# A seven-product pair kernel: negated products preset into PSUM by ScalarE, three banks in place of four, and another order of the products

## The chip, the cores and the metric

The kernel runs on one core of a Trainium2 chip. Times are device microseconds (us) of one execution. A comparison of two kernels uses runs of both on the same chip. PE is TensorE (matrix products), ACT is ScalarE, DVE is VectorE, POOL is GpSimd and SP is SyncE, which issues most transfers. Products are written to PSUM, an accumulator memory of eight banks per partition, from which ACT and DVE read.

## The reference

One layer of a hybrid decoder is computed for 512 prompt tokens and 64 sample tokens, so 576 token columns in all, with width 1024:

```python
h = _rmsnorm(x, norm1_g) * (1.0 + sc1) + sh1
proj = h @ w_in          # b_gate, c_gate, xa, q, k, v, ga, gb
ya = (b_gate * uc) @ w_conv_out          # uc: causal conv of c_gate * xa
yb = o @ w_attn_out                      # o: windowed attention of q, k, v
mixed = jax.nn.sigmoid(ga) * ya + jax.nn.sigmoid(gb) * yb
x = x + g1 * (mixed @ w_mix_out)
h2 = _rmsnorm(x, norm2_g) * (1.0 + sc2) + sh2
a, val = jnp.split(h2 @ w_up, 2, axis=-1)
ac, new_ffn = _causal_conv(a, ffn_buf, ffn_conv_w)
x = x + g2 * ((jax.nn.gelu(ac, approximate=False) * val) @ w_down)
```

The results are the normed outputs and the new convolution and key/value states. All arrays are float32.

## The kernel before, in words

Activations lie transposed in the core's memory: 128 features in the partitions, 576 tokens in the columns (`NT`, its half `HT` is 288). A weight tile covers 1024 input features and 128 output features. Every float32 operand is split in two: a high part, a rounded copy that ACT makes, and a low part, the remainder, that DVE makes (`split`, lines 135 to 138). A product is then three passes on PE: high by high, high by low, low by high.

The stages follow one another in the text of the kernel: norm and modulation, q, k, v, the short convolution with the attention woven in (`fill`, `tick`, lines 174 to 187), its output projection, the gates, the attention projection and merge, the mix projection, the second norm, the ConvFFN in three runs of weight tiles (`FCH`, line 28), each followed by its share of the down projection, and the final norm.

An ordinary product (`product`, lines 206 to 211) puts all 576 columns into one tile of two PSUM banks (`mmps`, a pool of two such tiles), in column groups of 256 and 320 (`GRP`, line 23; `halves`). Single banks come from `aux`, a pool of four.

Gates (16 weight tiles, 8 pairs) and most of the up projection (18 pairs of a value tile and a gate tile) are done by `pair_product` (lines 334 to 377). It treats the two weight tiles, their two input halves of 512 features and the two column halves of 288 as a two by two matrix product, and gets it with seven products of half size rather than eight. Sums and differences of the weights are made by DVE one pair ahead (`pair_weights`, lines 283 to 327: A, B, C, D stand for the split parts, such as `ah` for the high part of A and `al` for the low part), those of the activations once (`PairOperands`). Each of the seven parts is 12 matrix instructions of 288 columns into one bank. Parts write X, Y, Z, X, W, Y, Z. X and W are `aux` banks, Y and Z are two `mmps` tiles, each used in its first half bank alone. Between the parts, ACT copies part 1 and part 3 out of PSUM (`p1`, `p5`), DVE forms `u` and `v` (differences with `p1`), and the four results are formed by the functions `out_a0` to `out_b1` that the caller gives.

For the gates (`sigmoid_pair`, lines 1200 to 1219) these take the sigmoid. For the ConvFFN (`FfnPair.run`, lines 1520 to 1541) `value0` keeps X in PSUM, `value1` is a DVE subtraction, `gate0` and `gate1` write the padded gate tile `u` for the causal convolution, the last 64 columns by POOL. The convolution of one pair runs beside the products of the next: `first_tap` (ACT), `taps` (two DVE operations), `gelu` (ACT), `times` (DVE and POOL), `high` and `low` (the split of the result).

From the gates on, the instructions of PE, ACT and DVE are pinned to the order in which the text issues them (`InOrder`, lines 101 to 115, `pinned`), up to the last down projection (line 1737) with a break in the merge and mix stages. `in_turn` (lines 329 to 332) and `beside_pair` (lines 1561 to 1571) say after which part of a pair each split of the next weights and each convolution step of the pair before is issued. So an instruction that waits holds up all that stand behind it on its engine. Where two instructions touch the same tile, the tile framework puts a semaphore wait between them.

Of the kernel before, what the change touches and what calls it, by code (L numbers as in the profile page):

```python
# [12 lines left out]
AF = mybir.ActivationFunctionType  # L13
ALU = mybir.AluOpType
# [7 lines left out]
NT = SEQ + 64  # L22
GRP = [(0, 256), (256, 576)]
# [11 lines left out]
W_BUFS = 4  # L35
S_BUFS = 5
HT = NT // 2
NORM2 = 4, 0, 3, 1, 3
WARM = 2, 5
CND, CNS, CIND, CSL, CEND = 0, 256, 768, 772, 776  # L40
# [29 lines left out]
def step_kernel(ctx: ExitStack, tc: tile.TileContext, ins: dict, outs: list):  # L70
    nc = tc.nc
# [18 lines left out]
    def slot(s, dt=F32, shape=None):  # L90
        return ap_.tile(shape or [P, NT], dt, tag="a", name=nm(s))

    def mmps():
        return pm.tile([P, 1024], F32, tag="mm", name=nm("mm"))

    def aux():
        return pa.tile([P, 512], F32, tag="aux", name=nm("aux"))
# [16 lines left out]
    pe, act, dve, pool = (InOrder(e) for e in (nc.tensor, nc.scalar, nc.vector, nc.gpsimd))  # L114
    pinned += [pe, act, dve, pool]
    matmul, transpose = pe.matmul, pe.transpose
# [3 lines left out]
    def pf(ps):  # L120
        return ps[:, 256:832]
# [69 lines left out]
            if next(filler[0], True):  # L191
                filler.clear()

    def kstep(dst, w, xs, k, groups=(0, 1)):

        hi, lo = w
        xh, xl = xs[k]
        first, last = k == 0, k == len(xs) - 1
        for wt, x, st, sp_ in ((hi(k), xh, first, False), (hi(k), xl, False, False), (lo(k), xh, False, last)):
            for g in groups:  # L200
                matmul(dst[g], wt, x[:, GRP[g][0] : GRP[g][1]], start=st, stop=sp_)

    def halves(ps):
        return ps[:, 256:512], ps[:, 512:832]

    def product(w, xs):
        ps = mmps()
        for k in range(len(xs)):
            kstep(halves(ps), w, xs, k)
            tick()  # L210
        return pf(ps)

    def product_g(w, xs, g, bank=None, between=None):

# [113 lines left out]

    def in_turn(t):

        order = {0: "sums1 ah al", 2: "dh dl sums2", 3: "bh bl", 4: "ch cl"}
        return {at: (lambda names=names: [t[n]() for n in names.split()]) for at, names in order.items()}

    def pair_product(w, x, steps, out_a0, out_a1, out_b0, out_b1):

        X, Y, Z, W = (t[:, :HT] for t in (aux(), mmps(), mmps(), aux()))
        keep, uv = slot("p15"), slot("uv")
        p1, p5, u, v = keep[:, :HT], keep[:, HT:], uv[:, :HT], uv[:, HT:]  # L340

        def part(at, bank, wn, xn_, more=False):

            (hi, lo), xs = w[wn], x[xn_]
            for k in range(4):
                xh, xl = xs[k]
                passes = (hi(k), xh), (hi(k), xl), (lo(k), xh)
                for n, (wt, xx) in enumerate(passes):
                    matmul(
                        bank, wt, xx, start=not more and k + n == 0, stop=k + n == 5,  # L350
                        skip_group_check=more,
                    )
                tick()
            if at in (1, 3):
                act.copy(p1 if at == 1 else p5, bank)
            elif at == 2:
                dve.tensor_tensor(out=u, in0=Y, in1=p1, op=ALU.subtract)
            elif at == 4:
                out_a0(X)
            elif at == 6:  # L360
                dve.tensor_tensor(out=v, in0=Y, in1=p1, op=ALU.subtract)
                out_b0(v, W, ALU.add)
                out_b1(v, p5, ALU.subtract)
            elif at == 7:
                out_a1(Z, u, ALU.subtract)
            if at in steps:
                steps[at]()

        if 0 in steps:
            steps[0]()  # L370
        part(1, X, "a0", "x00")
        part(2, Y, "s2", "t2")
        part(3, Z, "s1", "n1")
        part(4, X, "a1", "x10", True)
        part(5, W, "b1", "n4")
        part(6, Y, "s3", "n3", True)
        part(7, Z, "s4", "x11", True)

    def kpm(w, m0, k0=0, nk=NK):
        return w[k0 * P : (k0 + nk) * P, m0 : m0 + P].rearrange("(k p) m -> p k m", p=P)  # L380
# [79 lines left out]
    part = cp.tile([P, 2, 8], F32, tag="part1", name="part1")  # L460
# [236 lines left out]
    for j in (2, 0, 1):  # L697
        t = slot("kT")
# [37 lines left out]
    for i in range(5):  # L736
        ps = aux()
# [11 lines left out]
    for i in (3, 4):  # L749
# [3 lines left out]
        t = slot("kout", shape=[P, 256])  # L753
# [21 lines left out]
    def queries(t, ps=None):  # L775
# [52 lines left out]
        out=sel,  # L828
        in0=snk.rearrange("p (h g) -> p h g", h=4),
        in1=ind.unsqueeze(1).to_broadcast([P, 4, 4]),  # L830
        op=ALU.mult,
# [331 lines left out]
    for m in range(NK):  # L1163
        if m in (5, 6):
            src, dst = ((ins["cache_k_win"], nks), (ins["cache_v_win"], nvs))[m - 5]
# [34 lines left out]
    def sigmoid_pair(w, steps):  # L1200

        sa, sb = slot("sg"), slot("sg")

        def a0(ps):
            act.activation(sa[:, :HT], ps, AF.Sigmoid)

        def a1(x, y, op):
            dve.tensor_tensor(out=sa[:, HT:], in0=x, in1=y, op=op)
            act.activation(sa[:, HT:], sa[:, HT:], AF.Sigmoid)

        def b0(x, y, op):
            dve.tensor_tensor(out=sb[:, :HT], in0=x, in1=y, op=op)

        def b1(x, y, op):
            dve.tensor_tensor(out=sb[:, HT:], in0=x, in1=y, op=op)
            act.activation(sb, sb, AF.Sigmoid)

        pair_product(w, made["op"], steps, a0, a1, b0, b1)
        return [sa, sb]
# [80 lines left out]
    def residual(ps, xt, blk, c0=0, c1=NT):  # L1300

        p1 = min(c1, 512)
        dve.scalar_tensor_tensor(
            out=xt[:, c0:p1], in0=ps[:, : p1 - c0], scalar=modT[:, blk, 0:1], in1=xt[:, c0:p1],
            op0=ALU.mult, op1=ALU.add,
        )
        if c1 > 512:
            t = sp.tile([P, 64], F32, tag="rt", name=nm("rt"))
            dve.tensor_tensor(
                out=b8(t), in0=b8(ps[:, p1 - c0 :]), in1=bc(modT[:, blk, 1:9]), op=ALU.mult  # L1310
            )
            dve.tensor_tensor(out=sv(xt), in0=sv(xt), in1=t, op=ALU.add)
# [196 lines left out]
    class FfnPair(FfnTile):  # L1509
# [10 lines left out]
        def run(self, steps):  # L1520
            self.u = u = padded()

            def value0(ps):
                self.x0 = ps

            def value1(x, y, op):
                self.x1 = y
                dve.tensor_tensor(out=y, in0=x, in1=y, op=op)

            def gate0(x, y, op):  # L1530
                dve.tensor_tensor(out=u[:, 2 : 2 + HT], in0=x, in1=y, op=op)

            def gate1(x, y, op):
                n = 512 - HT
                dve.tensor_tensor(out=u[:, 2 + HT : 514], in0=x[:, :n], in1=y[:, :n], op=op)
                nc.gpsimd.tensor_tensor(
                    out=b10(u)[:, :, 2:10], in0=b8(x[:, n:]), in1=b8(y[:, n:]), op=op
                )
                self.state()

            pair_product(self.w, made2["op"], steps, value0, value1, gate0, gate1)
# [19 lines left out]
    def beside_pair(p, t):  # L1561

        none = lambda: None
        f = lambda n: t[n] if t else none
        g = lambda n: getattr(p, n) if p else none
        return {
            0: [f("ah"), g("first_tap"), f("sums1"), f("al"), g("taps")],
            1: [f("dh"), f("bh"), g("gelu")],
            2: [f("dl"), f("sums2"), f("bl"), g("times")],
            4: [f("ch"), g("high"), f("cl"), g("low")],  # L1570
        }

# [114 lines left out]
    for m0, m1 in FCH:  # L1687
# [24 lines left out]
        if m1 < NF:  # L1712
            pairs = {m1: FfnPair(m1)}
            steps = None
            ps = [mmps() for _ in range(2)]
            n = m1 - m0
            for k0, k1 in ((0, n - 2), (n - 2, n)):
                for j in range(2):
                    for k in range(k0, k1):
                        kstep(halves(ps[j]), wd[j], fa, k)  # L1720
            wd[2] = split_w(down_load(2, m0, m1))
            for j in range(2):
                residual(pf(ps[j]), x1[j], 40 + j)
            for m in range(2, NK):
                if m + 1 < NK:
                    wd[m + 1] = split_w(down_load(m + 1, m0, m1))
                acc_m = product(wd[m], fa)
                if m == 4:
                    steps = in_turn(pairs[m1].prepare())
                    steps[0]()  # L1730
                elif m > 4:
                    steps[m - 3]()
                if m == NK - 1:
                    pairs[m1 + 1] = FfnPair(m1 + 1)
                residual(acc_m, x1[m], 40 + m)
            continue
# [32 lines left out]
        for k0, k1 in ((0, n - 2), (n - 2, n)):  # L1769
            for j in range(2):  # L1770
                for k in range(k0, k1):
                    kstep(halves(ps[j]), wd[j], fa, k)
        w = split_w(down_load(2, m0, m1))
        for j in range(2):
            residual(pf(ps[j]), x1[j], 40 + j)
            summed(j)
        for m in range(2, NK - LATE):
            acc_m = product(w, fa)
# [64 lines left out]
```

## Time and profile before

| What | Value |
| --- | --- |
| Time, median of 3 runs | 1001.54 us (1001.21 to 1002.3) |
| Span of the profiled execution, first to last instruction | 999.2 us |
| PE busy | 983.2 us, 98% of the span |
| DVE busy | 672.2 us, 67% |
| ACT busy | 449.6 us, 45% |
| POOL busy | 100.4 us, 10% |
| Chain that ended last, share of PE | 88% |
| Mean granted TensorE clock | 0.998 |

The profile is of one execution. Its page gives busy time by engine, the chain of work that ended last, and groups of instructions with their count, busy time, mean duration in ns and the idle time before them. The name before the arrow is the tile written, those behind it are read; `mm` and `aux` are PSUM tiles. Nearly all rows of PE, ACT and DVE carry the line of the helper that records them (L109), so tiles and shapes tell them apart. Windows give the busy time of each engine within a stretch, with the number of instructions, the granted clock, and the share and rate of the DMA engines. A timeline row gives start, duration, engine and, in brackets, idle time before it with what ended it.

### The profile page before, as it was taken

To read this page: it belongs to the slowest core of one execution; us is meant where nothing else is said; L and a number is where in the kernel's file an instruction comes from. 1 tells how busy PE (TensorE), PEld (TensorE's weight loads), DVE (VectorE), ACT (ScalarE), POOL (GpSimd) and SP (SyncE) were. 2 spreads that over 40 slices of the span, in tenths; PEclk is the share of its full clock that TensorE was granted. 3 is DMA by queue.
4 is the path that set the end of the run, shared out by engine and by line. 5 is a ranking of instruction groups with operands and counts; after the bars stand their busy time and mean duration, and the time that the engine had idled before them with its cause. 6 is when DMAs were issued, how large, how long until landed. Compare 5 with 4: busy or idle time off the path is not lost.

```text
span 999.2 us, 18724 instructions
## 1 busy us (share of the span) xinstructions
PE 983.2 (98%) x7516; PEld 942.1 (94%) x7516; DVE 672.2 (67%) x1243; ACT 449.6 (45%) x837; POOL 100.4 (10%) x271
## 2 busy tenths in 40 slices
PE   7999999999999999999999999999999999999997
PEld 6799999999989889999889999999999999999997
DVE  5637666666563367888454568896569995579954
ACT  5354545444544225545232347554225553235453
POOL 2222111100010000000000021011001110001120
PEclk9999999999999999999999999999999999999999
DMA  9983322333423822235972302233233222323302
GB/s 305 320 247 95 107 84 78 93 110 111 141 65 88 289 97 85 86 103 156 342 230 73 107 6 79 65 85 106 85 95 95 86 85 86 106 67 100 110 9 95
DMA packets 173481, 119.18 MB, mean 119 GB/s; under 512 B 6887, under 2 KB 160846, under 8 KB 173106
## 3 DMA queue, kind: packets, MB, share of 16 engines
q1 hardware_dynamic: 169954, 107.00, 35.1%
q0 software_dynamic: 3296, 10.73, 3.4%
q8 instruction: 59, 0.97, 0.4%
q14 instruction: 28, 0.23, 0.1%
q10 hardware_dynamic: 144, 0.26, 0.1%
HBM read 109.17 MB, written 7.35 MB: 117 GB/s over the span
## 4 chain that ended last, share of the span: by engine, by line
PE 88%; DVE 5%; ACT 2%; DMA 2%; issue 2%; SPq 0%; POOL 0%; POOLq 0%; DVEq 0%; ACTq 0%
PE mm L109 64%; PE aux L109 21%; PE aux L1104 2%; PE aux L1019 1%; DMA ad<-in_w_ada 1%; DVE wlo L109 1%; DMA raw<-in_w_in 1%; ACT whi L109 1%; SPq L385 0%; DVE raw L109 0%; DVE cy L109 0%; ACT y L109 0%; DVE uv L109 0%; DVE tl L109 0%; DVE fl L109 0%
## 5 line engine op out<-in xcount | busy, mean ns | idle before, releaser
L109 ACT ACTIVATE whi<-raw 128x1024 fp32r<-128x1024 f32 (+3 forms) x166 | 168.1, 1024 | 200.8 <-PE mm L109 106.9
L109 DVE TENSOR_TENSOR wlo<-raw,whi 128x1024 fp32r<-128x1024 f32 (+3 forms) x166 | 195.3, 1183 | 48.3 <-ACT whi L109 46.2
L109 PE MATMUL mm<-hh,whi 128*128 128x256 f32 (+2 forms) x560 | 127.6, 304 | 0.5 <-ACT hh L109 0.5
L109 PE MATMUL mm<-hh,wlo 128*128 128x256 f32 (+2 forms) x560 | 122.1, 295 | 0.0
L109 PE MATMUL mm<-hl,whi 128*128 128x256 f32 (+2 forms) x560 | 121.0, 295 | 0.1
L109 PEld LDWEIGHTS mm<-hh,whi 128*128 128x128 f32 x560 | 91.6, 188 | 8.1 <-issue 6.6
L109 PEld LDWEIGHTS mm<-hl,whi 128*128 128x128 f32 x560 | 93.7, 188 | 0.7 <-DVE hl L109 0.5
L109 PEld LDWEIGHTS mm<-hh,wlo 128*128 128x128 f32 x560 | 94.2, 188 | 0.0
L109 DVE SCALAR_TENSOR_TENSOR x<-mm,modT,x 128x512 f32<-128x512 f32 (+1 forms) x33 | 22.6, 686 | 70.6 <-PE mm L109 70.5
L109 PE MATMUL mm<-fl,whi 128*128 128x256 f32 (+1 forms) x304 | 65.4, 296 | 0.0
L109 PE MATMUL mm<-fh,whi 128*128 128x256 f32 (+1 forms) x304 | 64.8, 295 | 0.3 <-DVE rt L109 0.3
L109 PE MATMUL mm<-fh,wlo 128*128 128x256 f32 (+1 forms) x304 | 64.7, 294 | 0.0
L109 PE MATMUL mm<-th,whi 128*128 128x288 f32 x208 | 61.6, 296 | 0.7 <-DVE uv L109 0.7
L109 PE MATMUL mm<-th,wlo 128*128 128x288 f32 x208 | 61.4, 295 | 0.5 <-DVE wlo L109 0.5
L109 PE MATMUL mm<-tl,whi 128*128 128x288 f32 x208 | 61.2, 294 | 0.0
L109 PEld LDWEIGHTS mm<-fh,whi 128*128 128x128 f32 x304 | 50.6, 188 | 0.5 <-PE mm L109 0.5
L109 PEld LDWEIGHTS mm<-fh,wlo 128*128 128x128 f32 x304 | 51.0, 188 | 0.0
L109 PEld LDWEIGHTS mm<-fl,whi 128*128 128x128 f32 x304 | 50.9, 188 | 0.0
L109 PE MATMUL aux<-2h,whi 128*128 128x288 f32 (+2 forms) x160 | 47.3, 295 | 0.8 <-ACT p L109 0.8
L109 PE MATMUL aux<-2h,wlo 128*128 128x288 f32 (+2 forms) x160 | 47.2, 295 | 0.0
L109 PE MATMUL aux<-2l,whi 128*128 128x288 f32 (+2 forms) x160 | 47.0, 294 | 0.0
L870 ACT ACTIVATE s<-s,nmx 128x256 f32<-128x256 f32 (+1 forms) x72 | 34.1, 475 | 25.5 <-DVE nmx L867 17.4
(310 smaller groups left out, 2569.8 us busy)
## 6 DMA issues: line engine op xcount, KB each, us to landing
raw<-in_w_in SPq DMA_DIRECT2D x52, 512.0 KB, 4.2
raw<-in_w_up SPq DMA_DIRECT2D x44, 512.0 KB, 3.8
ada<-in_w_ada SPq DMA_DIRECT2D x64, 256.0 KB, 6.0
ad<-in_w_ada SPq DMA_DIRECT2D x32, 256.0 KB, 6.3
raw<-in_w_down SPq DMA_DIRECT2D x16, 512.0 KB, 3.5
raw<-in_w_conv_out SPq DMA_DIRECT2D x8, 512.0 KB, 3.5
raw<-in_w_attn_out SPq DMA_DIRECT2D x8, 512.0 KB, 3.5
raw<-in_w_mix_out SPq DMA_DIRECT2D x8, 512.0 KB, 5.6
```

The costliest lines, as they stand in the source:

```text
L109: done = getattr(self.engine, name)(*args, **kwargs)
L870: nc.scalar.activation(s[x // 2][:, x % 2, :w], s[x // 2][:, x % 2, :w], AF.Exp, bias=nmx[:, x : x + 1], accum_out=den[:, x : x + 1],)
L1019: done = nc.tensor.matmul(O[HALF[par], :256], vt(i - nkt + 1 + kt)[:, hd * 64 : hd * 64 + 64], pts[kt][:, par * 256 : par * 256 + 256], st ...
L1104: done = nc.tensor.matmul(ps[32 * j : 32 * j + 32, :], cT[:, k, :], cols[k][j], start=(k == 1), stop=(k == NK - 2),)
```

## The change

- Y and Z are now the two halves of one `mmps` tile (`even_halves`): the 288 columns before column 512 and the 288 columns from it on, one half in each of its two banks. W is gone, and with X a pair uses three banks. The slots `p1`, `u` and `v` are gone; only `p5` stays.
- The parts come in a new order and go to X, Z, Y, X, Y, Z, Y. After part 1 ACT writes the negated X into Y, and the products of part 3 add onto it. After part 3 ACT writes the negated Y into Z, and part 6 adds onto that. ACT still copies Z to `p5` after part 2.
- `b0` is now complete in Y after part 7 and read by ACT: a copy into `u` for the ConvFFN (`gate0`), a sigmoid for the gates. `b1` is a DVE subtraction after part 5, `a1` a DVE addition after part 6. The last 64 columns of `gate1` move from POOL to DVE.
- In the gates, the sigmoid of `sb` is done in two halves.
- The splits of the next weights are issued in another order (`in_turn`, `beside_pair`): B before D.
- Ordinary products and the first two down projections of each run use two even column groups of 288 (`EVEN`, `whole`).

```diff
+EVEN = [(0, HT), (HT, NT)]
...
-    def kstep(dst, w, xs, k, groups=(0, 1)):
+    def kstep(dst, w, xs, k, groups=(0, 1), at=GRP):
...
-                matmul(dst[g], wt, x[:, GRP[g][0] : GRP[g][1]], start=st, stop=sp_)
+                matmul(dst[g], wt, x[:, at[g][0] : at[g][1]], start=st, stop=sp_)
...
+    def even_halves(ps):
+        return ps[:, 512 - HT : 512], ps[:, 512 : 512 + HT]
+
+    def even_step(ps, w, xs, k):
+        kstep(even_halves(ps), w, xs, k, at=EVEN)
+
+    def whole(ps):
+        return ps[:, 512 - HT : 512 + HT]
...
-        order = {0: "sums1 ah al", 2: "dh dl sums2", 3: "bh bl", 4: "ch cl"}
+        order = {0: "sums1 ah al", 2: "bh bl sums2", 3: "dh dl", 4: "ch cl"}
...
-        X, Y, Z, W = (t[:, :HT] for t in (aux(), mmps(), mmps(), aux()))
-        keep, uv = slot("p15"), slot("uv")
-        p1, p5, u, v = keep[:, :HT], keep[:, HT:], uv[:, :HT], uv[:, HT:]
+        X = aux()[:, :HT]
+        Y, Z = even_halves(mmps())
+        p5 = slot("p5")[:, :HT]
...
-            if at in (1, 3):
-                act.copy(p1 if at == 1 else p5, bank)
-            elif at == 2:
-                dve.tensor_tensor(out=u, in0=Y, in1=p1, op=ALU.subtract)
-            elif at == 4:
-                out_a0(X)
-            elif at == 6:
-                dve.tensor_tensor(out=v, in0=Y, in1=p1, op=ALU.subtract)
-                out_b0(v, W, ALU.add)
-                out_b1(v, p5, ALU.subtract)
-            elif at == 7:
-                out_a1(Z, u, ALU.subtract)
...
+        def minus(out, src):
+            act.activation(out, src, AF.Copy, scale=-1.0)
+
+        parts = [
+            (X, "a0", "x00", lambda: minus(Y, X)),
+            (Z, "s1", "n1", lambda: act.copy(p5, Z)),
+            (Y, "s2", "t2", lambda: minus(Z, Y)),
+            (X, "a1", "x10", lambda: out_a0(X)),
+            (Y, "s3", "n3", lambda: out_b1(Y, p5, ALU.subtract)),
+            (Z, "s4", "x11", lambda: out_a1(Z, p5, ALU.add)),
+            (Y, "b1", "n4", lambda: out_b0(Y)),
+        ]
...
-            act.activation(sb, sb, AF.Sigmoid)
+        def a1(x, y, op):
+            sigmoid(sb[:, HT:], sb[:, HT:])
+            dve.tensor_tensor(out=sa[:, HT:], in0=x, in1=y, op=op)
+
+        def b0(ps):
+            sigmoid(sb[:, :HT], ps)
+            sigmoid(sa[:, HT:], sa[:, HT:])
...
-            def gate0(x, y, op):
-                dve.tensor_tensor(out=u[:, 2 : 2 + HT], in0=x, in1=y, op=op)
+            def gate0(ps):
+                act.copy(u[:, 2 : 2 + HT], ps)
...
-                nc.gpsimd.tensor_tensor(
+                dve.tensor_tensor(
                     out=b10(u)[:, :, 2:10], in0=b8(x[:, n:]), in1=b8(y[:, n:]), op=op
                 )
...
-            1: [f("dh"), f("bh"), g("gelu")],
-            2: [f("dl"), f("sums2"), f("bl"), g("times")],
+            1: [f("bh"), g("gelu")],
+            2: [f("bl"), f("sums2"), f("dh"), f("dl"), g("times")],
```

More of the change, by code (lines that the diff above doesn't have):

```diff
@@ L208, in product @@
         for k in range(len(xs)):
-            kstep(halves(ps), w, xs, k)
+            even_step(ps, w, xs, k)
             tick()
-        return pf(ps)
+        return whole(ps)
     def product_g(w, xs, g, bank=None, between=None):
@@ L329, in in_turn, with part @@
     def in_turn(t):
-        order = {0: "sums1 ah al", 2: "dh dl sums2", 3: "bh bl", 4: "ch cl"}
+        order = {0: "sums1 ah al", 2: "bh bl sums2", 3: "dh dl", 4: "ch cl"}
         return {at: (lambda names=names: [t[n]() for n in names.split()]) for at, names in order.items()}
     def pair_product(w, x, steps, out_a0, out_a1, out_b0, out_b1):
-        X, Y, Z, W = (t[:, :HT] for t in (aux(), mmps(), mmps(), aux()))
-        keep, uv = slot("p15"), slot("uv")
-        p1, p5, u, v = keep[:, :HT], keep[:, HT:], uv[:, :HT], uv[:, HT:]
-        def part(at, bank, wn, xn_, more=False):
+        X = aux()[:, :HT]
+        Y, Z = even_halves(mmps())
+        p5 = slot("p5")[:, :HT]
+        def part(bank, wn, xn_, more=True):
             (hi, lo), xs = w[wn], x[xn_]
@@ L353, in part @@
                 tick()
-            if at in (1, 3):
-                act.copy(p1 if at == 1 else p5, bank)
-            elif at == 2:
-                dve.tensor_tensor(out=u, in0=Y, in1=p1, op=ALU.subtract)
-            elif at == 4:
-                out_a0(X)
-            elif at == 6:
-                dve.tensor_tensor(out=v, in0=Y, in1=p1, op=ALU.subtract)
-                out_b0(v, W, ALU.add)
-                out_b1(v, p5, ALU.subtract)
-            elif at == 7:
-                out_a1(Z, u, ALU.subtract)
-            if at in steps:
-                steps[at]()
+        def minus(out, src):
[9 more added lines that the diff above has]
+        ]
         if 0 in steps:
             steps[0]()
[L371 to L377, printed above, removed]
+        for at, (bank, wn, xn_, after) in enumerate(parts):
+            part(bank, wn, xn_, at > 1)
+            after()
+            if at + 1 in steps:
+                steps[at + 1]()
     def kpm(w, m0, k0=0, nk=NK):
@@ L1202, in sigmoid_pair, with sigmoid @@
         sa, sb = slot("sg"), slot("sg")
+        def sigmoid(out, src):
+            act.activation(out, src, AF.Sigmoid)
         def a0(ps):
[L1205 to L1212, printed above, removed]
+            sigmoid(sa[:, :HT], ps)
         def b1(x, y, op):
             dve.tensor_tensor(out=sb[:, HT:], in0=x, in1=y, op=op)
-            act.activation(sb, sb, AF.Sigmoid)
+        def a1(x, y, op):
[4 more added lines that the diff above has]
+            sigmoid(sa[:, HT:], sa[:, HT:])
         pair_product(w, made["op"], steps, a0, a1, b0, b1)
@@ L1719, in step_kernel @@
                     for k in range(k0, k1):
-                        kstep(halves(ps[j]), wd[j], fa, k)
+                        even_step(ps[j], wd[j], fa, k)
             wd[2] = split_w(down_load(2, m0, m1))
             for j in range(2):
-                residual(pf(ps[j]), x1[j], 40 + j)
+                residual(whole(ps[j]), x1[j], 40 + j)
             for m in range(2, NK):
@@ L1771, in step_kernel @@
                 for k in range(k0, k1):
-                    kstep(halves(ps[j]), wd[j], fa, k)
+                    even_step(ps[j], wd[j], fa, k)
         w = split_w(down_load(2, m0, m1))
         for j in range(2):
-            residual(pf(ps[j]), x1[j], 40 + j)
+            residual(whole(ps[j]), x1[j], 40 + j)
             summed(j)
```

## The prediction

> **What bounds the kernel now.** I read the page first, then the windows over the pair stages, then single instructions there.
>
> ```profile
> span 999.2 us, 18724 instructions
> ...
> PE 983.2 (98%) x7516; PEld 942.1 (94%) x7516; DVE 672.2 (67%) x1243; ACT 449.6 (45%) x837; POOL 100.4 (10%) x271
> ```
>
> The span is 999.2 us against a median of 1001.54, so 2.3 us lie around it; I keep these. TensorE works almost without a pause. A change pays only by closing PE gaps, and costs whatever gaps it opens. The change sits in 26 pairs of weight tiles: 8 gate pairs (from about 380 us) and 18 ConvFFN pairs (three runs of 4, 8 and 6). The windows for one pair each (columns: PE, weight loads, DVE, ACT, POOL busy, then clock):
>
> ```profile
> 413.40:424.50 11.10, 11.10 (x86) 11.10 (x86) 9.04 (x13) 5.59 (x10) 0.00 (x0) 1.00 0.34 97
> ...
> 760.30:771.40 11.10, 11.10 (x86) 11.10 (x86) 10.97 (x17) 6.35 (x9) 1.42 (x5) 1.00 0.30 86
> ...
> 805.30:816.90 11.60, 11.30 (x86) 11.09 (x85) 11.46 (x19) 5.92 (x9) 1.76 (x6) 1.00 0.32 95
> ```
>
> A pair is 84 products and takes 11.1 us, 0.132 us a product. In ConvFFN pairs DVE is as full as PE, and late in a run the pair stretches. The chain in order of time gives the pair starts:
>
> ```profile
> 783.67 3.16 PE mm L109 x24
> ...
> 794.77 3.39 PE mm L109 x24
> ...
> 806.40 3.40 PE mm L109 x24
> ...
> 818.02 3.40 PE mm L109 x24
> ```
>
> 11.10, then 11.63 and 11.62: 0.5 us lost in such a pair. With the first pair of the first run (below) I put all that a lighter DVE could win at 3.5 us.
>
> **How one wait costs.** In the first ConvFFN pair PE already waits for a ScalarE copy of 288 columns, and a little later an unhindered copy follows its products (timeline):
>
> ```profile
> 646.24 0.37 ACT L109 COPY p<-aux 128x288 f32<-128x288 f32 x1
> ...
> 646.66 0.40 PE L109 MATMUL aux<-2h,whi 128*128 128x288 f32 x1 [0.84 <-ACT p L109]
> ...
> 646.90 0.29 PE L109 MATMUL aux<-2l,whi 128*128 128x288 f32 x1
> ```
>
> ```profile
> 750.07 0.29 PE L109 MATMUL aux<-2h,wlo 128*128 128x288 f32 x1
> 750.21 0.29 PE L109 MATMUL mm<-th,whi 128*128 128x288 f32 x1
> ```
>
> ```profile
> 750.40 0.40 ACT L109 COPY p<-aux 128x288 f32<-128x288 f32 x1 [1.04 <-PE aux L109]
> 750.70 0.64 ACT L109 ACTIVATE wh<-s 128x512 fp32r<-128x512 f32 x1
> ```
>
> Read: the copy starts 0.33 us after the start of the last product (750.07), lasts 0.40, and the next ACT operation begins 0.30 after it. PE restarts 0.05 after the copy's end (646.61 to 646.66) and its second product comes 0.24 later, not 0.13. So a product group that must wait for a copy of the group directly before it starts 0.33 + 0.40 + 0.05 - 0.13 = 0.65 us late, plus 0.11 for the restart: 0.76 us.
>
> **The change, part by part.** *New waits.* Y and Z become the two halves of one tile of two banks. In the program built from the changed kernel the products wait for the last access to the tile, not to their half. In all 26 pairs, with groups G1 to G7 in the new order (X, Z, Y, X, Y, Z, Y): G2 (Z) waits for the negated copy into Y; G3 (Y) waits for that and the copy of Z to p5; G5 (Y) for the negated copy into Z; G6 (Z) for the DVE reads of Y; G7 (Y) for the DVE read of Z. Only G5 has a whole group (G4, into X) to hide behind. Before, Y, Z, X and W are four tiles, and no such wait shows. Behind each wait stands all of PE's later work, in order.
>
> What PE waits for also stands in a queue, so durations matter (groups by line and form, mean ns after the comma):
>
> ```profile
> L109 DVE TENSOR_TENSOR wlo<-raw,whi 128x1024 fp32r<-128x1024 f32 x154 | 187.5, 1221 | 48.3 <-ACT whi L109 46.2 <-PE aux L109 1.6
> L109 ACT ACTIVATE whi<-raw 128x1024 fp32r<-128x1024 f32 x154 | 161.3, 1055 | 200.5 <-PE mm L109 106.9 <-DMA raw<-in_w_down 35.4 <-DVE raw L109 22.7
> ...
> L109 DVE SCALAR_TENSOR_TENSOR y<-pad,par2T,y 128x592 f32<-128x592 f32 x44 | 36.6, 833 | 4.9 <-ACT y L109 3.9
> ...
> L109 ACT ACTIVATE y<-pad,par2T 128x592 f32<-128x592 f32 x22 | 17.4, 792 | 32.7 <-POOL sto L1082 29.8 <-DVE pad L109 2.6
> L109 DVE TENSOR_TENSOR fl<-cy,fh 128x576 fp32r<-128x576 f32 x22 | 16.5, 752 | 5.2 <-ACT fh L109 5.2
> ...
> L109 ACT ACTIVATE y<-y 128x592 f32<-128x592 f32 x22 | 15.4, 699 | 30.7 <-DVE y L109 30.7
> ...
> L109 DVE TENSOR_TENSOR uv<-mm,uv 128x288 f32<-128x288 f32 x18 | 8.1, 452 | 1.4 <-PE mm L109 1.4
> L109 DVE TENSOR_TENSOR pad<-uv,p 128x224 f32<-128x224 f32 x18 | 6.9, 386 | 0.0
> ```
>
> *A full ConvFFN pair* (12 of the 18: a neighbour before and behind). Zero is the start of the last product of the pair before. Operations of one engine overlap by about 0.08 to 0.1, as above.
> - G1's last product starts at 1.59. ACT has meanwhile: the new copy of the gate out of Y (0.33), the high half of the next A (0.63 to 1.68), the first tap (to 2.37). Only then the negated copy, 2.28 to 2.68. G2 starts at 2.73, not 1.72: 1.01 lost.
> - G2's last starts at 4.29. The p5 copy stands behind the GELU, which needs the DVE's taps: low half of A from 1.73, taps 2.87 and 3.73 to 4.56, GELU 4.60, p5 5.20 to 5.60. G3 starts at 5.65, not 4.42: 1.23 lost.
> - G3's last 7.21; the negated copy into Z, 7.54 to 7.94, lies beside G4; G5 runs on, last product 10.38. 0 lost.
> - The DVE's gate operations on Y stand behind the low halves of C and of the pair before: ACT high C 8.99 to 10.04 (it needs the end of G4), low C to 11.31, the other low half to 11.97, then 0.39 and 0.20 on Y, done at 12.40. G6 starts at 12.45, not 10.51: 1.94 lost.
> - G7 waits for the in-place DVE add on p5: 0.33 + 0.45 + 0.05 - 0.13 = 0.70 lost.
>
> With four restarts of 0.11: 5.3 us a pair, 12 pairs: 64 us.
>
> *First and last pair of a run* (6): without a pair before there are no taps or GELU ahead of p5, and nothing but low C ahead of the gate: 0.65 + 0.65 + 1.27 + 0.70 + 0.44 = 3.7, three times: 11. The last has no next weights, so nothing but the next low half: 0.65 + 0.65 + 0.78 + 0.70 + 0.44 = 3.2, three times: 10.
>
> *Gate pairs* (8):
>
> ```profile
> L109 ACT ACTIVATE sg<-aux x8: 410/412/414, 391.1 to 468.0; 128x288 f32<-128x288 f32 x8
> ```
>
> G2 and G3 at 0.76 each, G7 at 0.81. After G4 come the sigmoid (0.33), high C 0.31 later (1.05), low C on DVE (1.74 to 2.96), and only then the add on Y, 2.88 to 3.33: G6 is 1.66 + 0.11 late. 4.1 us a pair: 33 us.
>
> *DVE relief.* In ConvFFN, three operations of 0.45 leave DVE and 0.20 comes in from POOL, in gate pairs three leave: beside PE, worth the 3.5 us above at most. If PE waits anyway, they go into the waits.
>
> *Even halves in ordinary products.* 256 + 320 columns become 288 + 288:
>
> ```profile
> L109 PE MATMUL mm<-th,whi 128*128 128x288 f32 x208 | 61.6, 296 | 0.7 <-DVE uv L109 0.7
> ...
> L109 PE MATMUL mm<-fh,wlo 128*128 128x320 f32 x152 | 46.8, 308 | 0.0
> ...
> L109 PE MATMUL mm<-fh,wlo 128*128 128x256 f32 x152 | 42.6, 280 | 0.0
> ```
>
> (308 + 280)/2 = 294 against 296: nothing. SP's DMA order is unchanged. The gate copy, now after the last group, delays the last run's tail by some 0.7 us.
>
> *Unknown: ScalarE writing PSUM.* No row shows it. Nearest are the 0.37 to 0.40 us copies out of PSUM and 0.64 for 512 columns; I take 0.40, and keep 0.2 and 0.64 as ends. It lies on the path once a pair: 26 x (-0.2 to +0.24) = -5 to +6 us.
>
> **Sum:** 64 + 11 + 10 + 33 = 118, less 3.5, plus 0.7: 115. The span goes to 1114, the median to 1116.5.
>
> **Rivals.** *Waits at their floor.* If the queues of ACT and DVE have drained when a group ends (PE being slower, they might), each of four waits costs 0.76 or 0.81: 3.1 x 26 = 81, less 3.5: 1079. Against it: the splits of C are held by the end of G4 itself. 8%.
>
> *Waits by bank.* If the waits on the other half were met early, only true dependences remain: gate copy, high A, taps, p5, copy into Z, gate operations, G7. The same chain then ends at 10.66 where G7 would start at 9.64, so about 1.1 us in 12 pairs: 13, less 3.5: 1011. 3%. The Trainium skill, "PSUM — Partial Sum Buffer" (section "PSUM bank collisions raise a hardware error"), says to guard PSUM by bank and quadrant, or simply by bank, rather than by address; by it the waits between Y and Z, in two banks, are needless and this rival would hold. The trace of before agrees as far as it goes: a copy out of one bank runs beside products into another at 750.40.
>
> *Faster.* The same, and the chain fits into G7's start: DVE's relief of 1.1 us closes the 3.5 us of gaps: 998. It decides if ACT does high A before the gate copy, which its order in the built program excludes. 2%.
>
> *The clock falls.* PE would idle 5 of 16 us. If the granted clock halved for a tenth of the 26 x 11.1 us of pair products, +29: 1145; for all of them, 1400.
>
> ```profile
> 0.00:10.00 10.00, 5.45 (x28) 4.99 (x29) 3.98 (x8) 6.66 (x15) 3.24 (x14) 1.00 0.76 244
> ```
>
> Against it: 1.00 here, with PE busy 5.45 of 10. 6%. The Trainium skill, "TensorE: Matmul & The Clock Gate" (section "What's actually happening"), has the gate close after an idle window of about 3.4 us; by it gaps of at most 2 us keep the clock, and the row agrees.
>
> **Numbers.** Forecast 1116, 81%. Range 1075 to 1145: the copy's ends, the floor, a tenth of clock loss. Only waits by bank, the faster case and a large clock loss lie outside. 0.2% (2 us) is about what a measurement can tell: slower 0.97, within 0.01, faster 0.02.
>
> **What would show it.** Right: in the windows a middle ConvFFN pair at about 16.4 us with PE busy 11 to 12, a gate pair at 15.2; PE waiting for ACT's mm and p5 and for DVE's pad, p5 and sg in all 26 pairs, 1.9 us at most; DVE below 70% there; product stages unchanged. Wrong: pairs of 11 to 12 us, or waits of 0.7 us only, or a clock under 1.

## The result, and the profile after

The changed kernel takes 1131.97 us (median of 5 runs, 1130.04 to 1140.43), the kernel before 1001.54 us on the same chip. The ratio is 1.132, with a 95% interval of 1.128 to 1.135. The profiled execution is the longest of the five: 1140.43 us with a mean granted clock of 0.972; the other four have 0.981 to 0.986.

The page of the changed kernel:

```profile
span 1138.5 us, 18682 instructions
...
PE 1032.7 (91%) x7516; PEld 968.4 (85%) x7516; DVE 646.9 (57%) x1183; ACT 465.2 (41%) x889; POOL 92.2 (8%) x253
...
PEclk9999999999999989999999998899988999989899
```

PE runs the same 7516 products, but is idle for 106 us instead of 16, and its busy time has grown by 50 us: the clock row shows eights, which the kernel before has none of in its pair stages. The windows of single pairs, from one pair's first product to the next one's (columns: PE, weight loads, DVE, ACT, POOL busy, clock, DMA):

```profile
450.02:465.28 15.26, 12.17 (x86) 11.23 (x85) 8.76 (x12) 6.09 (x11) 0.00 (x0) 1.00 0.23 69
...
747.00:800.00 53.00, 52.45 (x396) 52.38 (x396) 24.92 (x41) 13.37 (x15) 0.79 (x5) 1.00 0.29 85
815.04:833.28 18.24, 14.02 (x87) 12.96 (x86) 10.70 (x16) 6.85 (x11) 1.43 (x5) 0.87 0.19 58
884.96:901.39 16.43, 12.19 (x86) 11.26 (x85) 10.70 (x16) 6.85 (x11) 1.37 (x5) 1.00 0.22 65
800.15:815.04 14.89, 12.19 (x87) 11.25 (x85) 10.06 (x16) 3.85 (x6) 0.33 (x2) 1.00 0.25 72
676.96:699.65 22.69, 15.66 (x86) 14.61 (x85) 13.81 (x22) 7.91 (x14) 0.33 (x2) 0.77 0.32 94
```

A gate pair (450) takes 15.3 us, a middle ConvFFN pair (885) 16.4, the first pair of a run (800) 14.9: 11.1 each before. The down projection between two runs (747 to 800) is nearly as full as it was. Two rows show what comes on top: a pair in which the clock falls (815) takes 18.2 us, and the very first ConvFFN pair (677) 22.7 us. Seven middle pairs are of the first kind, with 17.7 to 18.9 us. The waits of PE (total us, times, longest):

```profile
PE mm L110 <- DVE pad L110: 26.1, 17, 1.8
PE mm L110 <- ACT p L110: 19.5, 26, 1.1
PE mm L110 <- ACT mm L110: 19.4, 25, 4.8
PE mm L110 <- DVE sg L110: 16.2, 16, 2.2
PE mm L110 <- DVE p L110: 9.9, 18, 0.6
```

None of these rows stands in the profile before. Their sum is 91 us, less than the 139 by which this execution's span is longer than that of the kernel before. A row counts from the end of the last product, which lies some 0.16 us behind the point where the next one would have started (the 0.84 us below make a group 1.00 us late): 16 us more in 102 waits. The restarts (0.11 each, 11 us) and the clock come on top.

The sizes within one pair, from the timeline of PE in the pair at 884.96 (start, duration; in brackets the idle time and what ended it):

```profile
886.41 0.29 PE L110 MATMUL aux<-2h,wlo 128*128 128x288 f32 x1
...
887.54 0.40 PE L110 MATMUL mm<-th,whi 128*128 128x288 f32 x1 [0.84 <-ACT mm L110]
...
889.10 0.29 PE L110 MATMUL mm<-th,wlo 128*128 128x288 f32 x1
...
890.46 0.40 PE L110 MATMUL mm<-th,whi 128*128 128x288 f32 x1 [1.06 <-ACT p L110]
...
895.22 0.29 PE L110 MATMUL mm<-2h,wl 128*128 128x288 f32 x1
...
897.31 0.40 PE L110 MATMUL mm<-2h,whi 128*128 128x288 f32 x1 [1.79 <-DVE pad L110]
...
898.86 0.29 PE L110 MATMUL mm<-2h,wlo 128*128 128x288 f32 x1
...
899.70 0.40 PE L110 MATMUL mm<-nh,whi 128*128 128x288 f32 x1 [0.55 <-DVE p L110]
```

Two products in a row start 0.13 us apart. Across the four waits it is 1.13, 1.36, 2.09 and 0.84, so G2, G3, G6 and G7 come 1.00, 1.23, 1.96 and 0.71 us late; the forecast had 1.01, 1.23, 1.94 and 0.70. No wait stands ahead of G5.

The clock, in four windows of 3.41 us (the length of its steps in the trace; all that fall in the pair stages last one, two or three of them):

```profile
825.15:828.56 3.41, 1.63 (x13) 1.39 (x12) 2.17 (x4) 0.39 (x1) 0.33 (x2) 1.00 0.30 88
828.56:831.97 3.41, 2.86 (x13) 2.51 (x12) 1.75 (x3) 0.00 (x0) 0.00 (x0) 0.50 0.23 68
```

```profile
842.21:845.62 3.41, 1.69 (x13) 1.45 (x11) 2.31 (x4) 1.63 (x2) 0.06 (x1) 1.00 0.15 43
845.62:849.03 3.41, 2.79 (x19) 2.57 (x20) 1.44 (x4) 0.00 (x0) 0.27 (x2) 1.00 0.53 153
```

After a window with PE busy for 1.63 us the clock is at half, after one with 1.69 it is not. Nine such falls hold 58 us of the pair stages. Half the clock costs half of that at most, 29 us, and less where PE waits anyway. This is the longest of the five executions; with a mean clock of 0.981 to 0.986 instead of 0.972 the others lost less.

### The profile page after: what moved, and what is told of

Read it like the earlier page. It is cut to its first block, busy times and chain, and to the rows that moved or that the text cites. A ratio compares the mean times of both kernels' runs of the same rounds, so it can differ in the third digit from the quotient of the medians.

```text
span 1138.5 us, 18682 instructions
## 1 busy us (share of the span) xinstructions
PE 1032.7 (91%) x7516; PEld 968.4 (85%) x7516; DVE 646.9 (57%) x1183; ACT 465.2 (41%) x889; POOL 92.2 (8%) x253
## 4 chain that ended last, share of the span: by engine, by line
PE 74%; DVE 11%; ACT 9%; issue 3%; DMA 2%; SPq 0%; POOL 0%; POOLq 0%; DVEq 0%; ACTq 0%
PE mm L110 59%; PE aux L110 13%; ACT whi L110 4%; DVE wlo L110 4%; DVE y L110 2%; PE aux L1110 1%; PE aux L1025 1%; DMA ad<-in_w_ada 1%; ACT p L110 1%; DVE fl L110 1%; DVE p L110 1%; ACT sg L110 1%; DVE pad L110 1%; DMA raw<-in_w_in 1%; DVE sg L110 1%
## 5 line engine op out<-in xcount | busy, mean ns | idle before, releaser
L110 PE MATMUL mm<-hh,whi 128*128 128x288 f32 (+2 forms) x560 | 128.8, 306 | 12.2 <-DVE sg L110 11.8
L110 PE MATMUL mm<-hh,wlo 128*128 128x288 f32 (+2 forms) x560 | 122.8, 296 | 0.0
L110 PE MATMUL mm<-hl,whi 128*128 128x288 f32 (+2 forms) x560 | 121.8, 296 | 0.1
L110 PEld LDWEIGHTS mm<-th,whi 128*128 128x128 f32 x208 | 40.1, 193 | 51.0 <-ACT p L110 25.7
L110 PE MATMUL mm<-2h,whi 128*128 128x288 f32 (+2 forms) x152 | 45.2, 323 | 26.1 <-DVE pad L110 26.1
L110 PE MATMUL mm<-fh,whi 128*128 128x288 f32 x304 | 65.2, 296 | 1.0 <-ACT pad L110 0.5
L110 PE MATMUL mm<-fl,whi 128*128 128x288 f32 x304 | 65.0, 295 | 0.0
L110 PE MATMUL mm<-fh,wlo 128*128 128x288 f32 x304 | 64.9, 295 | 0.0
L110 PEld LDWEIGHTS mm<-2h,whi 128*128 128x128 f32 x152 | 29.2, 201 | 30.1 <-DVE pad L110 30.1
L110 PE MATMUL mm<-nh,whi 128*128 128x288 f32 x104 | 37.3, 359 | 14.3 <-DVE p L110 9.9
```

The source lines that it names most:

```text
L110: done = getattr(self.engine, name)(*args, **kwargs)
```

## The experiments

Nine kernels, in the order in which they were run. For a view of the whole first the periods of a pair, from first product to first product, where the clock is undisturbed:

| Kernel | Time, us | Gate pair | Middle ConvFFN pair |
| --- | --- | --- | --- |
| before | 1001.5 | 11.1 | 11.1 |
| changed | 1132.0 | 15.3 | 16.4 |
| two tiles | 1028.8 | 11.8 | 12.3 |
| even halves alone | 1002.7 | 11.1 | 11.1 |
| gate's reads first | 1102.2 | 14.4 | 15.3 |
| dummy products in the waits | 1123.5 | 15.3 | 16.4 |
| one tile, old order | 1073.0 | 12.8 | 14.1 |
| two tiles, other columns | 1028.3 | 11.8 | 12.3 |
| two tiles, gate's reads first | 1008.1 | 11.1 | 11.2 |
| the same, four edits more | 1002.3 | 11.2 | 11.2 |

**Y and Z in two tiles.** The theory: the waits come from the tile that Y and Z share.

```diff
-        Y, Z = even_halves(mmps())
+        Y, Z = (mmps()[:, :HT] for _ in range(2))
```

> The changed kernel with one edit: Y and Z come from two separate tiles instead of being the two halves of one. Products, their order, the negated copies and the even halves stay. Of the five waits between the groups of a pair only the true ones remain: the third group for the negated copy into Y, the fifth for the negated copy into Z, the seventh for the gate's reads. Theory (the shared tile makes the waits, and the waits let the clock fall): the granted clock is back at 1.00 in the pair stages, a middle ConvFFN pair takes at most 12.3 us instead of 16.4, a gate pair 11.1 to 11.3 instead of 15.3, and the time is about 1011 us (1003 to 1018). Rival (the negated copies and the new order cost the time by themselves, with ScalarE's chain of sums, taps and GELU ahead of them): pairs stay above 14 us and the time above 1080 us.

1028.81 us, ratio 1.027 (1.026 to 1.028). 103 of the 130 us are gone with this one line, so the theory holds, and the rival (over 1080) falls. The number was missed by 18 us, though. Of that the trace shows: G7 still waits for the gate's reads (10.6 us in 13 waits for `pad`, 3.0 us in 7 for `sg`), which makes gate pairs 11.8 instead of 11.1 to 11.3; PE waits 3.7 us for the `ada` weights behind the gates, and 6.8 us of half clock follow; the first ConvFFN pair takes 15.8 us against 13.0 before. One thing more: this kernel computes something else. Its output for the prompt and the prompt's ConvFFN state are wrong, those of the samples, which lie in columns 224 to 287 of their half, are not. Read from that, and shown by no trace: the first pair of each ConvFFN run lost ScalarE's negated values in columns 0 to 223 of Y. The instructions and their order are the same, and the time can be read. The run with other columns takes it up.

**Even halves alone.** In the kernel before, only the column groups of the ordinary products change.

```diff
-            kstep(halves(ps), w, xs, k)
+            even_step(ps, w, xs, k)
```

> The kernel before with one part of the change: the ordinary products and the first two down projections run in groups of 288 and 288 columns instead of 256 and 320. The pairs stay as before. Theory: no difference, 1001.5 us within 2 us, because the mean of the 256 and 320 rows (294 ns) is that of the 288 row (296 ns). Rival (the even halves carry the 1.7 us by which the changed kernel's first gate pair starts later, 385.12 instead of 383.45 us): 1003 to 1005 us, and the first gate pair at about 385 us.

1002.66 against 1001.40 us, ratio 1.0012 (1.0003 to 1.0021). The size is within the 2 us of the theory, yet the rival's place was right: the first gate pair starts at 385.39 us instead of 383.45. Of these 1.94 us, 0.57 are there by the 300th product; the traces scatter by -0.36 to 0.74 us at this place, whatever their columns. From there to the first gate pair all seven traces with even halves fall behind the kernel before by 1.36 to 1.38 us, and the one in which the old columns come back (the last run) by 0.02. "Nothing" was some 1.3 us.

**The gate's reads first.** The shared tile stays; DVE does the gate's operations on Y and Z ahead of the low halves of C and of the pair before.

```diff
-            4: [f("ch"), g("high"), f("cl"), g("low")],
+            4: [f("ch"), g("high")],
+            5: [f("cl"), g("low")],
```

> The changed kernel with one edit: VectorE does the low half of C, and that of the previous pair, behind the gate's reads of Y and Z instead of ahead of them. The shared tile and all its waits stay. Theory (a wait costs what stands in the queue ahead of the operation waited for): the wait of the sixth group falls from 1.94 to about 0.84 us in a ConvFFN pair and from 1.66 to about 0.70 us in a gate pair, together about 22 us; with the shorter gaps part of the clock's loss of about 17 us goes too: 1093 to 1112 us, a middle ConvFFN pair at about 15.3 us and a gate pair at about 14.3 us. Rival (TensorE waits for the end of the group before and the engine's reaction only, whatever the queue holds): 1132 us, pairs as in the changed kernel.

1102.22 us, ratio 1.100 (1.099 to 1.102): 29.8 us less than the changed kernel. Its waits of PE:

```profile
PE mm L110 <- ACT mm L110: 20.8, 25, 4.8
PE mm L110 <- ACT p L110: 20.6, 26, 1.1
PE mm L110 <- DVE pad L110: 11.5, 17, 0.7
PE mm L110 <- DVE p L110: 9.4, 17, 0.6
PE mm L110 <- DVE sg L110: 8.9, 16, 0.7
```

The two DVE rows `pad` and `sg` fall from 26.1 + 16.2 to 11.5 + 8.9, by 21.9 us (22 forecast); the others stay. What a wait costs is what its engine has queued ahead of the awaited operation. The other 8 us fit the clock: the mean of the timed runs is 0.992 instead of 0.981 to 0.986, and the only fall in the pair stages is in the first ConvFFN pair.

**Dummy products in the waits.** The missing 16 us above the forecast: is it the clock? Products of the identity into a bank of their own, which nobody reads, fill the waits.

```diff
+            keep_warm(D, (0, 2, 2, 0, 0, 5, 2)[at])
             part(bank, wn, xn_, at > 1)
```

> The changed kernel with dummy products of the identity, whose results nobody uses, issued ahead of the second, third, sixth and seventh group of each pair (2, 2, 5 and 2 of them, about 0.22 us each), in a bank of their own: TensorE runs them while it would wait. The waits between the groups stay as they are. Theory (the time above the forecast, 1132 against 1116 us, is the granted clock, which falls to half in nine stretches of 3.4 to 10.2 us of the changed kernel's trace): the clock is 1.00 in all pair stages, no ConvFFN pair takes over 17 us, and the time is 1112 to 1120 us. Rival (the clock falls for another reason, or the missing time is in the waits): 1130 us or more, with half clock in the trace.

1123.54 us (1123.04 to 1124.48), 8.4 less than the changed kernel, although it issues 572 matrix instructions more. The pairs, and the first ConvFFN pair:

```profile
462.13:477.40 15.27, 14.65 (x108) 13.88 (x107) 9.03 (x13) 6.08 (x11) 0.00 (x0) 1.00 0.23 70
856.88:873.29 16.41, 14.62 (x108) 13.86 (x107) 10.70 (x16) 6.85 (x11) 1.44 (x5) 1.00 0.22 65
673.95:694.38 20.43, 15.96 (x109) 15.38 (x107) 13.80 (x22) 7.90 (x14) 0.33 (x2) 0.92 0.36 104
```

Every pair but one keeps its full clock, and most gate pairs and all middle pairs have the length that undisturbed pairs of the changed kernel have. So the clock is at least 8 us of the miss, and the theory was right in kind. Between the two profiled executions it is 17.4 us (1140.43 against 1123.04), since the changed kernel's was the one with the lowest clock. The forecast of this run was 3.5 us too low, and the last row has that: in the first ConvFFN pair PE waits 4.4 us for ScalarE's negated copy (4.8 in the changed kernel), which stands behind two splits of weights, the split of the last single tile and four copies of `n3`, and that third split itself waits 2.0 us for DVE's `cy`. One window of half clock follows. The forecast allowed 13.0 + 3.7 = 16.7 us for this pair; it takes 20.4.

**One tile in the old order.** The converse of the first experiment: the kernel before, with Y and Z in one tile and nothing else.

```diff
-        X, Y, Z, W = (t[:, :HT] for t in (aux(), mmps(), mmps(), aux()))
+        X, W = (aux()[:, :HT] for _ in range(2))
+        pair = mmps()
+        Y, Z = pair[:, 512 - HT : 512], pair[:, 512 : 512 + HT]
```

> The kernel before with one edit: Y and Z of a pair are the two halves of one tile, as in the changed kernel, instead of two tiles. The old order of the seven products, VectorE's sums and W stay; no bank is preset. In the program built from it the third group (Z) waits for VectorE's u out of Y, the sixth (Y) for ScalarE's p5 out of Z, the seventh (Z) for VectorE's reads of Y. Theory (the shared tile by itself makes most of the loss): three waits a pair with their queues, 0.8 to 1.9 us each, so 26 pairs of 13.5 to 15 us and 1060 to 1100 us. Rival (the loss belongs to the negated copies and the new order): within 5 us of 1001.5.

1073.01 us, ratio 1.072 (1.070 to 1.073). A single row holds it:

```profile
PE mm L109 <- DVE uv L109: 51.2, 51, 5.0
```

In the kernel before the same row is this:

```profile
PE mm L109 <- DVE uv L109: 0.7, 3, 0.3
```

51 waits, all for `u` or `v`, where the kernel before has three short ones: two a pair, not the three expected (none is for `p5`), and gate pairs of 12.8 us are under the 13.5 given. So the shared tile costs 72 us even without negated copies, its loss of clock (mean 0.985 to 0.988) included. The changed kernel has 102 waits of this kind, twice as many: in its order four groups of a pair wait.

**Two tiles, other columns.** Y and Z again in two tiles, but in the columns that the ordinary products write too.

```diff
-        Y, Z = (mmps()[:, :HT] for _ in range(2))
+        Y, Z = (even_halves(mmps())[0] for _ in range(2))
```

> As the run with Y and Z in two tiles, but both in the columns 224 to 511 of a bank, which the ordinary products with even halves write too, instead of columns 0 to 287. In the run with columns 0 to 287 the first pair of each run of ConvFFN tiles lost what ScalarE had put into columns 0 to 223 of Y: the products overwrote it there instead of adding. Theory for that (the last ordinary product opened the bank with a start and wrote columns 224 to 511 alone, and ScalarE's write does not end that state in the other columns): nothing is lost here. Time by the theory of the shared tile: a middle ConvFFN pair 12.29 us and a gate pair 11.81 us as there, and 1024 to 1029 us; the 3.7 us wait for the ada weights behind the gate pairs may or may not come again. Rival (the loss was a missing wait, which other columns would not mend): the same columns of a later read are wrong again.

1028.31 us, ratio 1.027 (1.026 to 1.029), and here nothing is lost: the theory of the open columns holds, and a missing wait as the cause falls, since the waits are the same in both. The pairs are as before, and the wait behind the gates comes again:

```profile
PE mm L110 <- DVE pad L110: 10.5, 13, 0.9
...
PE aux L1110 <- DMA ada<-in_w_ada: 3.5, 1, 3.5
PE mm L110 <- DVE sg L110: 3.0, 7, 0.6
```

**Two tiles and the gate's reads first.** The edits of the last kernel and of the third together.

> The run before this one together with VectorE's low half of C behind the gate's reads of Y and Z. In the two-tile run the seventh group's wait for the gate's reads (VectorE's pad and sg) was the only one left: 0.8 us in a middle ConvFFN pair and 0.4 us in a gate pair, plus restarts. Theory (the low half of C ahead of the gate is all of it): the wait goes, a middle ConvFFN pair takes 11.1 to 11.3 us and a gate pair 11.1 to 11.2 us, clock 1.00, and the time is 998 to 1006 us, equal to the kernel before or a little under it. Rival (the chain of ScalarE, with the negated copies ahead of sums and taps, is the limit behind it): pairs stay above 11.8 us and the time above 1015 us.

1008.13 us, ratio 1.008 (1.006 to 1.009). The rows `pad` and `sg` are gone, and the pairs are full:

```profile
430.07:441.20 11.13, 11.13 (x86) 11.13 (x85) 7.72 (x11) 6.20 (x11) 0.00 (x0) 1.00 0.34 97
790.36:801.57 11.21, 11.21 (x86) 11.19 (x85) 10.55 (x17) 6.88 (x11) 2.60 (x5) 1.00 0.32 96
646.43:661.09 14.66, 11.69 (x86) 11.23 (x85) 13.07 (x22) 7.72 (x14) 0.33 (x2) 1.00 0.38 108
```

The rival (ScalarE's chain) falls. The time is 2 us over the range given, and the full pairs are not the reason. The first ConvFFN pair gives 1.6 us (14.7 against 13.0 before), and the `ada` wait 3.4 us, with a window of half clock behind it. GpSimd's two loads of `x` stand as follows, in the kernel before and in this one:

```profile
474.92 0.57 POOL L1331 DMA_DIRECT2D x<-xT_dram  x1 [147.18 <-DVE ol L109]
479.14 0.53 POOL L1331 DMA_DIRECT2D x<-xT_dram  x1 [3.65 <-DMA ada<-in_w_ada]
```

```profile
474.61 0.57 POOL L1340 DMA_DIRECT2D x<-xT_dram  x1 [144.75 <-DVE ol L110]
478.52 0.54 POOL L1340 DMA_DIRECT2D x<-xT_dram  x1 [3.33 <-DVE ol L110]
```

Counted from the first product behind the gate pairs (472.60 and 474.57) the first goes out after 0.04 us instead of 2.32; it waits for DVE's `ol`, and DVE has less to do. The other two kernels with two tiles have 0.05 us and an `ada` wait of 3.5 and 3.7 us; the kernel with even halves alone has 2.31 us and none. The loads take the DMA engines from the `ada` weights in a stretch where these are full anyway (DMA share 1.02 from 480 to 490 us).

**Four edits more.**

```diff
-        Y, Z = (even_halves(mmps())[0] for _ in range(2))
+        Z, Y = (halves(mmps())[1][:, :HT] for _ in range(2))
...
-            beside = [{0: n3}] if m == 4 else []
+            beside = [{1: n3}] if m == 4 else []
...
+        nc.gpsimd.tensor_copy(out=x1t[x][:, 0, 0:1], in_=mixed[2][1].bitcast(F32)[:, 0:1])
         nc.gpsimd.dma_start(x1t[x], xT_dram[x])
```

(and the even halves taken back)

> From the run with two tiles and the gate's reads first, whose 1008.1 us stand 6.9 us above the kernel before. Its trace shows where: 3.4 us of waiting for the ada weights behind the gate pairs with 3.4 us of half clock right after, because GpSimd's load of x (2.4 MB) goes out 2.4 us earlier against the pairs and takes the DMA engines first; 1.6 us more in the first ConvFFN pair, where Z takes the bank that VectorE's cy still reads and the negated copy stands behind eight ScalarE copies of n3; about 2 us in the ordinary products ahead of the gate pairs. Four edits, one for each: x is loaded behind a one-element copy out of the third mixed tile; Y and Z change places in the order in which they take their tiles; n3 is made behind the first group; Y and Z lie in columns 512 to 799 of their tiles, which the ordinary products write with the old 256 and 320 columns, so the even halves go back. Theory: 3.4 + 1.7 + 1.6 + 1 to 2 us come back, first ConvFFN pair at most 13.0 us, 998 to 1001.5 us: the kernel before or up to 0.3% under it. Rival (the seven products with negated copies keep a cost of their own in the start of each run): 1003 us or more.

1002.34 against 1001.08 us, ratio 1.0014 (1.0005 to 1.0023). This is 0.8 us over the range given and under the rival's 1003. The `ada` wait and its half clock are gone: the loads of `x` go out at 501.30, and the longest `ada` load from 440 us on lands after 7.0 us instead of 12.1. The four edits were made together, so that the late load is the cure rests on these numbers. With the old columns the gate stage starts at 384.15 instead of 385.55. The first ConvFFN pair still takes 14.0 us, with 1.8 us of waiting for `cy`: changing the places of Y and Z did not help there, and why is not settled. A middle pair stays at 11.2 instead of 11.1. With its waits taken out, the change is about a microsecond from the kernel before; none of these versions beats it.

## Why the prediction was right and where it was short

The forecast was 1116 us in a range of 1075 to 1145; measured are 1132. The loss of 130 us was forecast as 115.

- *Direction and mechanism* were right: the waits are those read from the built program, in the pairs named, on the operations named, and removing the shared tile removes them.
- *The full ConvFFN pair* (5.3 us): four waits within 0.02 us of their forecast, period 16.43 against 16.4. *First pair of a run*: 14.9 against 14.8 in two of three runs. *Gate pair*: 15.26 against 15.2. *ScalarE writing PSUM*: taken as 0.40 us, measured 397 and 395 ns in two groups of 26.
- *Queue ahead of the awaited operation*: right, shown by moving two DVE operations (21.9 us of waits against 22).
- *Even halves, "nothing"*: 1.3 us (0.3 to 2.1). Why the even groups take longer is not shown.
- *"The clock falls"*, 6%, is the step that failed. The forecast kept the full clock and added no term for it; measured are 8 us at least between the changed kernel and the one with dummy products, and "a clock under 1", one of its own signs of being wrong, came. It had two arguments. One was a row of 10 us at the start of the kernel, with PE busy for 5.45 at a clock of 1.00. This clock was not measured: the clock records of that trace begin at 12.5 us, and the profile shows 1.00 where it has none. The products tell another clock:

```profile
7.70 5.15 PE L109 MATMUL aux<-ident,x 128*128 128x128 f32 x24
12.69 0.61 PE L109 MATMUL aux<-ident,rs 128*128 128x128 f32 x4
```

Products of the same size start 0.21 us apart up to 12.4 us and 0.11 us apart from there on, so PE ran at about half speed in the row that was to show full speed. The other argument was the rule of an idle window of 3.4 us that the prediction cites, read as one unbroken gap. In the pair stages of the changed kernel no wait but one is longer than 2.2 us, and the clock falls nine times.
- *The first ConvFFN pair*, sized as the other first pairs with 3.7 us: some 6 us without its half clock (20.4 - 1.7 - 13.0, the one cold window taken as 1.7). The rows were there in the trace of the kernel before, from 640.29 to 646.24: ACT has three long splits and four copies (not eight, as an expectation above says) queued where the negated copy is issued.
- *The sum.* Of the 15.5 us between 1116.5 and 1132.0, 8.4 are the clock, about 2 the first ConvFFN pair's waits, up to 1.7 its half clock that the dummy products left, 1.3 the even halves. Some 2 us are not assigned.
- *Rivals.* Waits at their floor (1079) did not come: G3 and G6 are 1.2 and 2.0 us late against its 0.8. Waits by bank (1011) is the two-tile kernel in deed, at 1028: its 1.1 us for a middle pair were right (1.18), but it took gate pairs as free (0.7 each) and did not see the late `ada` weights. "Faster" (998) has no version here.

## What to carry to other kernels

A memory tile is what the framework waits for, so two accumulators that are written and read in turns belong in two tiles, even where they lie in two banks: 103 us here for one line. Where a wait can't be avoided, look at what its engine has queued ahead of the awaited operation and move that behind it; and add up how busy TensorE is left in each stretch of a few microseconds, since short waits close together also cost the clock. Before a row's clock serves as evidence, compare the spacing of its products with that of the same products elsewhere. A faster stage frees buffers earlier, and the transfer that this starts may hit one that was just in time.

## What the runs showed of the hardware that was not expected

*In the pair stages the clock goes by the busy share of fixed windows.* On a grid of 3.41 us fixed by the steps of the clock in the trace of after, the nine full-speed windows of the pair stages after which the clock halved had PE busy for 0.09 to 0.48 of the time; all those after which it stayed had 0.49 or more. The two pairs of rows above (1.63 and 1.69 us) are the nearest on both sides. In the kernel with one tile in the old order six windows of 0.47 to 0.50 were followed by half clock, and none of 0.53 or more. In the kernel with the gate's reads first no window of the pairs but one lies under 0.54, and the clock falls once there. The dummy products' trace has one exception, a window of 0.44 without a fall, so the edge is not sharper than some 0.05; a busy PE in these records is partly modelled. At the start of the kernel, where the products are small, the share does not decide: windows of 0.50 to 0.64 were followed by half clock in six traces, one of 0.50 and one of 0.60 in two others were not. Why is open. The Trainium skill, "TensorE: Matmul & The Clock Gate" (section "HAM oscillation — how this bites in real kernels"), gives the rule as no idle gaps over about 3.4 us; the trace does not agree, since eight of the nine falls have no such gap. The same page (section "A second HAM failure mode: psum-queue depth-cycling") tells of a kernel whose short idle times between groups made the clock swing, and that is what this one does; the prediction did not weigh it.

*ScalarE's values are not always added to.* With Y in columns 0 to 287 the first pair behind an ordinary product lost them in columns 0 to 223, as read from the outputs; with Y in columns 224 to 511 it lost none. The ordinary products with even halves start in columns 224 to 511 of that bank and leave the others untouched. The Trainium skill, "PSUM — Partial Sum Buffer" (section "The four PSUM rules"), says that a starting product clears the written marks of its whole bank, that ScalarE's writes do not set them, and that a product without a start overwrites where the mark is clear. Both runs agree. It also gives the even halves of the change a reason that no time could show: they mark all columns that Y will use.
